# DeltaNet cores with full 128x128 inverses, built in two steps, and memory keys and values kept in DRAM between uses

## The chip, the cores and the metric

The kernel runs on one core of a Trainium2 chip. The metric is device time in microseconds (us). The profile is one more execution of the program, taken by the hardware profiler; its lines number the file of the kernel that was profiled.

## The reference

Two layers of a decoder trunk over 256 tokens with 2048 features, all in f32. Layer 0 mixes tokens with an mLSTM, layer 1 with a gated DeltaNet; each then attends to 256 memory tokens (4 heads of 128) and runs a dense MLP of width 8192 with squared ReLU. Each of the six sub-layers is `x + RMSNorm(f(RMSNorm(x)))`. What the change touches is the DeltaNet (32 value heads, 16 key heads, dimension 128, chunks of 64 tokens) and the attention's keys and values, which are made once from `mem` and used in both layers:

```python
A = jnp.einsum('...id,...jd->...ij', kb, kc) * jnp.exp(jnp.where(strict, diff, -jnp.inf))
U = lax.linalg.triangular_solve(A, vb, left_side=True, lower=True, unit_diagonal=True)
W = lax.linalg.triangular_solve(A, kb * jnp.exp(gam)[..., None], left_side=True, lower=True, unit_diagonal=True)
...
def step(Sst, xs):
    u_, w_, qg_, kd_, aqk_, dl_ = xs
    vn = u_ - jnp.einsum('bhld,bhde->bhle', w_, Sst)
    o = jnp.einsum('bhld,bhde->bhle', qg_, Sst) + jnp.einsum('bhls,bhse->bhle', aqk_, vn)
    Sst = dl_[..., None, None] * Sst + jnp.einsum('bhld,bhle->bhde', kd_, vn)
    return Sst, o
```

With 256 tokens the kernel needs no state: each head solves one unit lower triangular system over the tokens and multiplies the solution by the lower triangle of decayed q k products.

## The kernel before

**The work as a whole.** Nearly all of it is products of a 256-token activation with weights that are streamed from DRAM. Class `Weights` loads units of 512x512 (or 2048x128, "tall") in two halves on SP's queue (L74), rounds each on ACT (`hi`, L88) and takes the rest on DVE (`lo`, L89); TensorE (PE) then runs three products per block, hi·hi, lo·hi and hi·lo. Two units are kept ahead, in two buffers each of `hi` and `lo`. `prod_tok` (L378 to L380) has tokens in the output's partitions, `prod_feat` and `prod_tall` features.

**Order.** The program is written as one sequence; a scheduler then puts the instructions of each engine in an order of their own, by its estimate of when each can run. Each engine works its list off strictly in order. `behind` adds an order without a wait.

**The DeltaNet.** Stage gd1 makes q, k and the decays, and for each group of 4 value heads (8 groups) the matrices `at`: for each head three 128x128 blocks of the key system (token half 0 with itself, half 1 with itself, half 0 to half 1) and three of the query products. They go to DRAM (`at_d`), and the 32x32 diagonal blocks of the key system to `a_d`. Stage gd2 makes v, and beside it `solve` inverts the 32x32 blocks on DVE, all at once, one block a partition (`tm`); inverses go to DRAM as `t_d`, laid out in 64x64 with a zero off-diagonal quarter, and a transposed copy of the first of each pair to `tn_d`.

Stage gd3 is where the change works. For each group `core(grp, zs, ys)` runs behind the product gz of that group (`prod_tok`, 96 matmuls of 128x512, four weight units). Partitions are the 128 tokens of a half, `c2` is the chunk of 64 in it, `tt` the half, `hh` the head in the group. A core before:

- Loads, on POOL's queue: `vt` (values; L1083), `ti` (inverses, two loads; L1087), `ab` (the `at` matrices; one buffer, L1089), `tn` (one buffer, two loads; L1096).
- `np` (L1103, 16 matmuls 64x64 with 32 columns), a scaling on DVE (L1105), `xp` (L1114, 16 matmuls 32x32), two copies on ACT (L1118): this completes each 64x64 inverse.
- Then block substitution over the four chunks: `wp` (L1145) is the 64x64 inverse times the chunk's values, copied into `vt` on ACT (L1148); `cp` is what a solved chunk takes off the next one, within a half with 64x64 matmuls (L1139), from half 0 to half 1 with 128x128 ones (L1131); `minus` (L1124) subtracts it on DVE.
- `op` (L1156, 12 matmuls of 128x128) is the output; then a norm, the gate `zs`, four transposes `otp` (L1179), and the split of the result for the product g_out.

The scheduler has put gz matmuls of the next group between the steps of a core, so that PE works while ACT and DVE evacuate.

**Keys and values of the memory.** `kmT` (L522) and `vm` (L523) are made at the start and stay in two tiles of the pool `const` until the attention of layer 1; `cross` reads them at `xs` (L751) and `xop` (L775).

Of the kernel before, what the change touches and what calls it, by code (L numbers as in the profile page):

```python
# [7 lines left out]
F32 = mybir.dt.float32  # L8
F32R = mybir.dt.float32r
AF = mybir.ActivationFunctionType  # L10
ALU = mybir.AluOpType
# [3 lines left out]
P = 128  # L15
# [95 lines left out]
def trunk(ctx: ExitStack, tc, x, mem, norm_g, mem_norm_g, w_mem_kv, w_xq, w_xo, w_up, w_down,  # L111
# [295 lines left out]
    def new_u(n=KB):  # L407
        return [acts.tile([P, 2 * T], F32R, tag=f"u{k}", name=f"u{k}") for k in range(n)]
# [438 lines left out]
    def gdn(g0, h, rms):  # L847
# [4 lines left out]
        tn_d = tc.dram_tile([P, 64, 32], F32, name="tn_d")  # L852
# [175 lines left out]
        with tc.tile_pool(name="gd2", bufs=1) as sc:  # L1028
            def solve():


                rki = sc.tile([P, 2, 1, 32], F32, name="rki")
                nc.gpsimd.dma_start(rki, rk_d.rearrange("r v (c i) -> (r v c) i", c=2))
                tm = sc.tile([P, 64, 64], F32, name="tm")
                clear = G.memset(tm, 0.0)
                G.memset(tm.rearrange("p c i -> p (c i)")[:, 0:4096:65], 1.0)
                work = g0.tile([P, 2560], F32, tag="at", name="solve_w")
                am = work[:, 0:2048].rearrange("p (s j i) -> p s j i", s=2, j=32)
                pv = work[:, 2048:].rearrange("p (s c) -> p s c", s=2)
                zero = acts.tile([P, 32, 32], F32, tag="y1", name="zero")  # L1040
# [18 lines left out]
                tn = acts.tile([P, 32, 32], F32, tag="y0", name="tn")  # L1059
                S.copy(tn, td[0].rearrange("p c i -> p i c"))  # L1060
                nc.gpsimd.dma_start(tn_d[:, 0:32, :], tn)


            solver, steps = solve(), {3: 12, 4: 8, 5: 6, 6: 6}
            next(solver)
            for c in range(2, 8):
                prod_v(c)
                n = steps.get(c, 0)
                try:
                    for i in range(n):  # L1070
                        solver.send(padded[i * 4 // n - 4])
                except StopIteration:
                    pass
                store_v(c - 1)
        gp_stack.close()

        with tc.tile_pool(name="gd3", bufs=1) as sc:
            post = Post(1, 1)

            def core(grp, zs, ys):  # L1080

                vt = sc.tile([P, 2, 512], F32, tag="vt", bufs=2, name="vt")
                nc.gpsimd.dma_start(vt, v_d[grp])  # L1083
                ti = sc.tile([P, 2, 4, 64], F32, tag="ti", bufs=2, name="ti")
                for tt in range(2):
                    base = (tt * GV_H + grp * 4) * 2
                    nc.gpsimd.dma_start(ti[:, tt], t_d[base : base + 8].rearrange("(g c) j i -> (c j) g i", c=2))  # L1087
                ab = g0.tile([P, 6, 4, P], F32, tag="at", name="ab")
                nc.gpsimd.dma_start(ab, at_d[grp])  # L1089
                aa, aq = ab[:, 0:3], ab[:, 3:6]  # L1090
                w = vt

                tn = sc.tile([P, 2, 4, 32], F32, tag="tn", name="tn")
                for tt in range(2):
                    base = (tt * GV_H + grp * 4) * 2
                    nc.gpsimd.dma_start(tn[:, tt], tn_d[base : base + 8].rearrange("(g c) i j -> (c i) g j", c=2))  # L1096
                np_ = psum("np")
                for tt in range(2):
                    for c2 in range(2):
                        r_ = slice(c2 * 64, c2 * 64 + 64)  # L1100
                        for hh in range(4):
                            c = (tt * 4 + hh) * 32
                            PE.matmul(np_[r_, c : c + 32], aa[r_, tt, hh, r_], tn[r_, tt, hh, :],  # L1103
                                      start=(tt == 0 and hh == 0), stop=(tt == 1 and hh == 3), skip_group_check=True)
                V.tensor_tensor(tn.rearrange("p t (k v) i -> p t k (v i)", k=2),  # L1105
                                np_[:, 0:T].rearrange("p (t k i) -> p t k i", t=2, k=2),
                                nrk[:, :, grp * 2 : grp * 2 + 2].unsqueeze(3).to_broadcast([P, 2, 2, 64]), ALU.mult)
                xp = psum("xp")
                for tt in range(2):
                    for c2 in range(2):  # L1110
                        r1, r2 = slice(c2 * 64, c2 * 64 + 32), slice(c2 * 64 + 32, c2 * 64 + 64)
                        for hh in range(4):
                            c = (tt * 4 + hh) * 32
                            PE.matmul(xp[r1, c : c + 32], tn[r2, tt, hh, :], ti[r2, tt, hh, 32:64],  # L1114
                                      start=(tt == 0 and hh == 0), stop=(tt == 1 and hh == 3), skip_group_check=True)
                for c2 in range(2):
                    r1 = slice(c2 * 64, c2 * 64 + 32)
                    S.copy(ti[r1, :, :, 32:64], xp[r1, 0:T].rearrange("p (t h i) -> p t h i", t=2, h=4))  # L1118

                def minus(r_, tt, cp):  # L1120
                    for kh in range(2):
                        s_ = slice(kh * T, kh * T + T)
                        hk = grp * 2 + kh
                        V.scalar_tensor_tensor(vt[r_, tt, s_], cp[r_, s_], nrk[r_, tt, hk : hk + 1], vt[r_, tt, s_],  # L1124
                                               ALU.mult, ALU.add)

                for tt in range(2):
                    if tt == 1:
                        cp = psum("cp")
                        for hh in range(4):  # L1130
                            PE.matmul(cp[:, hh * P : (hh + 1) * P], aa[:, 2, hh, :], w[:, 0, hh * P : (hh + 1) * P],  # L1131
                                      start=(hh == 0), stop=(hh == 3), skip_group_check=True)
                        minus(slice(0, P), 1, cp)
                    for c2 in range(2):
                        r_ = slice(c2 * 64, c2 * 64 + 64)
                        if c2 == 1:
                            cp = psum("cp")
                            for hh in range(4):
                                PE.matmul(cp[64:128, hh * P : (hh + 1) * P], aa[0:64, tt, hh, 64:128],  # L1139
                                          w[0:64, tt, hh * P : (hh + 1) * P], start=(hh == 0), stop=(hh == 3),  # L1140
                                          skip_group_check=True)
                            minus(r_, tt, cp)
                        wp = psum("wp")
                        for hh in range(4):
                            PE.matmul(wp[r_, hh * P : (hh + 1) * P], ti[r_, tt, hh, :],  # L1145
                                      vt[r_, tt, hh * P : (hh + 1) * P], start=(hh == 0), stop=(hh == 3),
                                      skip_group_check=True)
                        S.copy(w[r_, tt, :], wp[r_])  # L1148

                ops = []  # L1150
                ss = sc.tile([P, 2, 4], F32, tag="ss", bufs=2, name="ss")
# [86 lines left out]
```

## Time and profile before

| | us |
|---|---|
| median of 3 runs | 2954.86 |
| lowest and highest run | 2952.91, 2958.61 |
| the profiled execution | 2962.7 |
| its span | 2960.6 |
| PE busy in it | 2911.2 (98%) |
| DVE busy | 1746.1 (59%) |
| ACT busy | 1443.7 (49%) |

The page lists busy time by engine (PEld is PE's loading of the stationary operand), the chain of work that ended last, groups of instructions by line, and DMA issues. In a line of the chain or the timeline the first number is the start in us from the beginning of the span, the second the length; `<-` names what was waited for. A busy PE isn't PE at its peak.

### The profile page before, as it was taken

Reading aid. Unit: us, or ns where it says so; the run is one execution under the profiler, and the core shown is the slowest. Engines: PE = TensorE matmul, PEld = TensorE weight load, DVE = VectorE, ACT = ScalarE, POOL = GpSimd, SP = SyncE. Lnnn points to the kernel's source line nnn. Section 1 sums busy time; section 2 is a strip of 40 time slices with the busy share of each in tenths; the row PEclk is TensorE's granted clock in tenths of the full one; section 3 lists DMA queues with packets and bytes.
Section 4 is the critical chain, followed back from the end, with each engine's and each line's share of the span. In section 5 each row is a group of like instructions: output and inputs, shape, how many; then the busy total and the mean of one; then the engine's idle time right before and its main releaser. Section 6 shows DMA issues by size and latency. Waiting matters only on the chain.

```text
span 2960.6 us, 42191 instructions
## 1 busy us (share of the span) xinstructions
PE 2911.2 (98%) x16595; PEld 2504.0 (85%) x16595; DVE 1746.1 (59%) x2544; ACT 1443.7 (49%) x2213; POOL 137.1 (5%) x256
## 2 busy tenths in 40 slices
PE   8999999999999999999999999999999999999998
PEld 7888888988888888898889977877888888888887
DVE  5555657654645555677778844444567546455565
ACT  6444546544434444566664544444456444344343
POOL 0000000000000000013321011000000000000000
PEclk9999999999999999999999999999999999999999
DMA  7545565556655556556778755655445565555565
GB/s 232 178 157 158 192 199 167 168 186 194 189 189 187 193 186 196 180 150 167 204 204 226 240 200 182 212 182 172 162 149 185 186 197 185 191 191 189 188 190 170
DMA packets 373960, 553.15 MB, mean 187 GB/s; under 512 B 22769, under 2 KB 155378, under 8 KB 371458
## 3 DMA queue, kind: packets, MB, share of 16 engines
q1 hardware_dynamic: 363456, 507.12, 55.1%
q0 software_dynamic: 8736, 42.02, 4.1%
q8 instruction: 130, 2.13, 0.3%
q10 hardware_dynamic: 1570, 1.33, 0.1%
q14 instruction: 68, 0.56, 0.1%
HBM read 527.29 MB, written 23.10 MB: 186 GB/s over the span
## 4 chain that ended last, share of the span: by engine, by line
PE 92%; DMA 3%; DVE 3%; ACT 1%; issue 1%; DVEq 0%; ACTq 0%; SPq 0%
PE up L314 15%; PE up L315 8%; PE down L378 8%; PE down L380 8%; PE down L379 8%; DMA raw<-in_gdn_w_in 2%; PE gz L378 2%; PE gz L380 2%; PE gz L379 2%; PE g_out L378 2%; PE g_out L380 2%; PE g_out L379 2%; PE o L314 2%; PE gv L335 2%; PE gv L333 2%; PE gv L334 2%
## 5 line engine op out<-in xcount | busy, mean ns | idle before, releaser
L89 DVE TENSOR_TENSOR lo<-raw,hi 128x1024 fp32r<-128x1024 f32 x938 | 1121.4, 1224 | 901.3 <-ACT hi L88 900.4
L88 ACT CAST hi<-raw 128x1024 fp32r<-128x1024 f32 x938 | 947.6, 1046 | 972.2 <-PE down L380 310.8
L314 PE MATMUL up<-h,hi 128*128 128x512 f32 x1920 | 678.7, 399 | 0.0
L315 PE MATMUL up<-h,lo 128*128 128x256 f32 x1920 | 539.2, 281 | 0.0
L314 PEld LDWEIGHTS up<-h,hi 128*128 128x128 f32 x1920 | 360.8, 188 | 89.8
L379 PE MATMUL down<-lo,u 128*128 128x512 f32 x1024 | 398.4, 389 | 0.0
L378 PE MATMUL down<-hi,u 128*128 128x512 f32 x1024 | 398.4, 389 | 0.0
L380 PE MATMUL down<-hi,u 128*128 128x512 f32 x1024 | 398.3, 389 | 0.0
L315 PEld LDWEIGHTS up<-h,lo 128*128 128x128 f32 x1920 | 362.7, 189 | 0.2
L380 PEld LDWEIGHTS down<-hi,u 128*128 128x128 f32 x1024 | 192.2, 188 | 40.0
L378 PEld LDWEIGHTS down<-hi,u 128*128 128x128 f32 x1024 | 192.2, 188 | 40.0
L379 PEld LDWEIGHTS down<-lo,u 128*128 128x128 f32 x1024 | 192.2, 188 | 39.6
L333 PE MATMUL gv<-h,hi 128*128 128x256 f32 x512 | 148.6, 290 | 1.7 <-ACT hi L88 1.7
L335 PE MATMUL gv<-h,lo 128*128 128x256 f32 x512 | 147.9, 289 | 0.8 <-DVE lo L89 0.8
L334 PE MATMUL gv<-h,hi 128*128 128x256 f32 x512 | 147.6, 288 | 0.0
L378 PE MATMUL gz<-hi,h 128*128 128x512 f32 x256 | 103.7, 405 | 0.0
L380 PE MATMUL gz<-hi,h 128*128 128x512 f32 x256 | 103.0, 402 | 0.0
L333 PEld LDWEIGHTS gv<-h,hi 128*128 128x128 f32 x512 | 100.7, 197 | 2.7 <-ACT hi L88 2.3
L379 PE MATMUL gz<-lo,h 128*128 128x512 f32 x256 | 102.5, 400 | 0.0
L335 PEld LDWEIGHTS gv<-h,lo 128*128 128x128 f32 x512 | 100.6, 197 | 1.5 <-DVE lo L89 1.5
L334 PEld LDWEIGHTS gv<-h,hi 128*128 128x128 f32 x512 | 100.8, 197 | 0.3 <-issue 0.2
L378 PE MATMUL g_out<-hi,u 128*128 128x512 f32 x256 | 100.9, 394 | 0.0
(412 smaller groups left out, 4728.4 us busy)
## 6 DMA issues: line engine op xcount, KB each, us to landing
raw<-in_w_up SPq DMA_DIRECT2D x256, 512.0 KB, 3.9
raw<-in_w_down SPq DMA_DIRECT2D x256, 512.0 KB, 4.2
raw<-in_gdn_w_in SPq DMA_DIRECT2D x192, 512.0 KB, 4.9
raw<-in_mlstm_w_in SPq DMA_DIRECT2D x96, 512.0 KB, 4.0
raw<-in_gdn_w_out SPq DMA_DIRECT2D x64, 512.0 KB, 4.2
raw<-in_mlstm_w_out SPq DMA_DIRECT2D x32, 512.0 KB, 4.4
at_d<-at POOLq DMA_DIRECT2D x8, 1536.0 KB, 7.6
ab<-at_d POOLq DMA_DIRECT2D x8, 1536.0 KB, 8.6
```

What stands on the lines that cost most here:

```text
L88: a = nc.scalar.copy(h_, raw[:, :, :n])
L89: return a, nc.vector.tensor_tensor(l_, raw[:, :, :n], h_, ALU.subtract)
L314: PE.matmul(a[:fw], wh, srcs[kk][:, :], start=(kk == 0), stop=False, skip_group_check=True)
L315: PE.matmul(a[:fw, T:], wl, srcs[kk][:, 0:T], start=False, stop=(kk == nk - 1), skip_group_check=True)
L333: PE.matmul(a[:, 0:T], hi[k], srcs[k][:, 0:T], start=(k == 0), stop=False)
L334: PE.matmul(a[:, 0:T], hi[k], srcs[k][:, T:], start=False, stop=False)
L335: m = PE.matmul(a[:, 0:T], lo[k], srcs[k][:, 0:T], start=False, stop=(k == nk - 1))
L378: PE.matmul(accs[t], sh, hi[j], start=(kk == 0), stop=False)
L379: PE.matmul(accs[t], sh, lo[j], start=False, stop=False)
L380: PE.matmul(accs[t], sl, hi[j], start=False, stop=(kk == nk - 1))
```

## The change

Instead of substituting over four chunks, each core completes the inverse of a whole half (128 tokens) and applies it once. The quarter step fills the 32x32 off-diagonal block of each 64x64 inverse (np, xp, now with 32x32 matmuls, and for the first chunk also its transposed form), the half step the 64x64 off-diagonal block of the 128x128 inverse (np, xp, 64 columns, eight matmuls each). wp is then one block of four 128x128 matmuls for each half, and only the cp from half 0 to half 1 is left. The full inverses lie in two tiles `tf` that are kept for the stage, with the lower left blocks cleared once; `tn` gets two buffers and four loads, `tf` four loads.

To make room, `kmT` and `vm` are stored to DRAM after they are made and their pool is closed; `cross` loads them into tiles of its own. The rest of the diff:

```diff
-    kmT = const.tile([P, XA_H, T], F32, name="kmT")
-    vm = const.tile([P, 2, 512], F32, name="vm")
+    km_d = tc.dram_tile([P, XA_H * T], F32, name="km_d")
+    vm_d = tc.dram_tile([P, 2 * 512], F32, name="vm_d")
+    kv_stack = ExitStack()
+    kv = kv_stack.enter_context(tc.tile_pool(name="kv", bufs=1))
+    kmT = kv.tile([P, XA_H, T], F32, name="kmT")
+    vm = kv.tile([P, 2, 512], F32, name="vm")
...
+    nc.gpsimd.dma_start(km_d, kmT.rearrange("p h m -> p (h m)"))
+    nc.gpsimd.dma_start(vm_d, vm.rearrange("p m d -> p (m d)"))
+    kv_stack.close()
...
     def cross(sc, l, h, rms):
...
+        kmT = sc.tile([P, XA_H, T], F32, bufs=1, name="kmT")
+        nc.gpsimd.dma_start(kmT.rearrange("p h m -> p (h m)"), km_d)
+        vm = sc.tile([P, 2, 512], F32, bufs=1, name="vm")
+        nc.gpsimd.dma_start(vm.rearrange("p m d -> p (m d)"), vm_d)
...
-                nc.gpsimd.dma_start(tn_d[:, 32:, :], zero)
+                nc.gpsimd.dma_start(tn_d[:, 0:32, 32:], zero)
+                nc.gpsimd.dma_start(tn_d[:, 32:, 0:32], zero)
...
-                S.copy(tn, td[0].rearrange("p c i -> p i c"))
-                nc.gpsimd.dma_start(tn_d[:, 0:32, :], tn)
+                for i in range(2):
+                    S.copy(tn[i], td[i].rearrange("p c i -> p i c"))
+                    r_ = slice(i * 32, i * 32 + 32)
+                    nc.gpsimd.dma_start(tn_d[:, r_, r_], tn[i])
...
+            tfs = [sc.tile([P, 2, 4, P], F32, name=f"tf{i}") for i in range(2)]
+            for tf in tfs:
+                G.memset(tf[64:, :, :, 0:64], 0.0)
...
+                        nc.gpsimd.dma_start(tf[r_, tt, :, r_],
+                                            t_d[base : base + 8].rearrange("(g c) j i -> c j g i", c=2)[c2])
...
-                            PE.matmul(np_[r_, c : c + 32], aa[r_, tt, hh, r_], tn[r_, tt, hh, :],
+                            PE.matmul(np_[q2[c2], c : c + 32], aa[q1[c2], tt, hh, q2[c2]], tn[q1[c2], tt, hh, 0:32],
...
+                        for c2 in range(2):
+                            t2 = tf[q2[c2], tt, hh, q2[c2]]
+                            PE.matmul(xp[q1[c2], c : c + 32], na_[q2[c2], c : c + 32], t2, **at_end)
+                        PE.matmul(xp[q2[0], c : c + 32], tf[q2[0], tt, hh, q2[0]], na_[q2[0], c : c + 32], **at_end)
+                x4 = lambda r_: xp[r_, 0:T].rearrange("p (t h i) -> p t h i", t=2, h=4)
+                V.tensor_copy(tn[q2[0], :, :, 0:32], x4(q2[0]))
                 for c2 in range(2):
+                    S.copy(tf[q1[c2], :, :, q2[c2]], x4(q1[c2]))
+                np_ = psum("np")
+                xp = psum("xp")
+                for tt in range(2):
+                    for hh in range(4):
+                        c = (tt * 4 + hh) * 64
+                        PE.matmul(np_[half[1], c : c + 64], aa[half[0], tt, hh, half[1]], tn[half[0], tt, hh, :],
+                                  start=(tt == 0 and hh == 0), stop=(tt == 1 and hh == 3), skip_group_check=True)
+                na_ = tmp.tile([P, 512], F32, tag="pair", bufs=3, name="na")
+                V.tensor_tensor(na_[half[1]].rearrange("p (t k i) -> p t k i", t=2, k=2),
+                                np_[half[1]].rearrange("p (t k i) -> p t k i", t=2, k=2),
+                                nrk[half[1], :, grp * 2 : grp * 2 + 2].unsqueeze(3).to_broadcast([64, 2, 2, P]), ALU.mult)
...
+                        PE.matmul(xp[half[0], c : c + 64], na_[half[1], c : c + 64], tf[half[1], tt, hh, half[1]],
+                                  start=(tt == 0 and hh == 0), stop=(tt == 1 and hh == 3), skip_group_check=True)
+                S.copy(tf[half[0], :, :, half[1]], xp[half[0]].rearrange("p (t h i) -> p t h i", t=2, h=4))
...
-                    for c2 in range(2):
-                        r_ = slice(c2 * 64, c2 * 64 + 64)
-                        if c2 == 1:
-                            cp = psum("cp")
...
-                                PE.matmul(cp[64:128, hh * P : (hh + 1) * P], aa[0:64, tt, hh, 64:128],
...
-                            PE.matmul(wp[r_, hh * P : (hh + 1) * P], ti[r_, tt, hh, :],
-                                      vt[r_, tt, hh * P : (hh + 1) * P], start=(hh == 0), stop=(hh == 3),
-                                      skip_group_check=True)
-                        S.copy(w[r_, tt, :], wp[r_])
+                    wp = psum("wp")
+                    for hh in range(4):
+                        PE.matmul(wp[:, hh * P : (hh + 1) * P], tf[:, tt, hh, :], vt[:, tt, hh * P : (hh + 1) * P],
+                                  start=(hh == 0), stop=(hh == 3), skip_group_check=True)
+                    S.copy(w[:, tt, :], wp)
```

The order of the instructions outside the cores is the same on PE, and nearly so on the other engines. Three places differ in a way that matters. The first is PE in the second core, from the cp between the halves to op. Before (the numbers tell buffers apart; hi and lo with one number are one weight unit):

```order
L1131 MATMUL cp<-vt,ab 128x128 x4
L380 MATMUL gz_1_16329<-hi_16148,h_10277 128x512
L378 MATMUL gz_1_16329<-hi_16148,h_10278 128x512
L379 MATMUL gz_1_16329<-lo_16149,h_10278 128x512
L1145 MATMUL wp<-vt,ti 64x128 x4
```

And in the change:

```order
L378 MATMUL gz_0_16366<-hi_16368,h_10293 128x512
L1170 MATMUL cp<-vt,ab 128x128 x4
L379 MATMUL gz_0_16366<-lo_16369,h_10293 128x512
L380 MATMUL gz_0_16366<-hi_16368,h_10293 128x512
L378 MATMUL gz_0_16366<-hi_16368,h_10294 128x512
L379 MATMUL gz_0_16366<-lo_16369,h_10294 128x512
L380 MATMUL gz_0_16366<-hi_16368,h_10294 128x512
L378 MATMUL gz_0_16366<-hi_16368,h_10295 128x512
L379 MATMUL gz_0_16366<-lo_16369,h_10295 128x512
L380 MATMUL gz_0_16366<-hi_16368,h_10295 128x512
L1179 MATMUL wp<-vt,tf_15744 128x128 x4
L1189 MATMUL op<-vt,ab 128x128 x12
```

Three gz matmuls lay between cp and the next wp; now eight do, the first of a new weight unit lies before cp, and op follows the second wp in one piece.

The second is DVE in the same core, from the scaling of np (lo is a weight split). Before:

```order
L1105 TENSOR_TENSOR tn<-np,nrk 128x256
L89 TENSOR_TENSOR lo_16331<-raw_0_16332,hi_16330 128x1024
L89 TENSOR_TENSOR lo_16331<-raw_2_16334,hi_16330 128x1024
L1124 SCALAR_TENSOR_TENSOR vt<-cp,nrk,vt 64x256 x2
L1124 SCALAR_TENSOR_TENSOR vt<-cp,nrk,vt 128x256 x2
L1124 SCALAR_TENSOR_TENSOR vt<-cp,nrk,vt 64x256 x2
```

And in the change:

```order
L1131 TENSOR_TENSOR na<-np,nrk 32x256 x2
L89 TENSOR_TENSOR lo_16369<-raw_0_16370,hi_16368 128x1024
L1145 COPY tn<-xp 32x8x32
L89 TENSOR_TENSOR lo_16369<-raw_2_16372,hi_16368 128x1024
L1156 TENSOR_TENSOR na<-np,nrk 64x512
L89 TENSOR_TENSOR lo_16403<-raw_0_16404,hi_16402 128x1024
L1175 SCALAR_TENSOR_TENSOR vt<-cp,nrk,vt 128x256 x2
L89 TENSOR_TENSOR lo_16403<-raw_2_16406,hi_16402 128x1024
```

Both splits of a unit stood together before the first subtraction; now one stands ahead of each of three steps of the core, the last of them (unit 16403) ahead of the subtraction between the halves.

The third is ACT at the end of layer 0's attention, where the norm's statistics of xo are taken (junk is the square's unused result, rpost the norm's factor). Before:

```order
L228 ACTIVATE junk,sspost<-xo_1_4430 128x512
L88 CAST hi_4493<-raw_0_4495 128x1024
L228 ACTIVATE junk,sspost<-xo_0_4491 128x512
L481 ACTIVATE rpost<-rpost,eps_t 128x1
L228 ACTIVATE junk,sspost<-xo_1_4492 128x512
```

And in the change:

```order
L911 ACT_TABLE_LOAD
L911 ACTIVATE na<-na 128x32
...
L88 CAST hi_4507<-raw_0_4509 128x1024
L228 ACTIVATE junk,sspost<-xo_0_4505 128x512
L481 ACT_TABLE_LOAD
L481 ACTIVATE rpost<-rpost,eps_t 128x1
```

The exponential of gdn_a_log (na), which stood in the mLSTM before, has moved into this place; a table load stands ahead of it and another one right ahead of rpost.

More of the change, by code (lines that the diff above doesn't have):

```diff
@@ L851, in gdn @@
         a_d = tc.dram_tile([P, 2, 32, 32], F32, name="a_d")
-        tn_d = tc.dram_tile([P, 64, 32], F32, name="tn_d")
+        tn_d = tc.dram_tile([P, 64, 64], F32, name="tn_d")
         t_d = tc.dram_tile([P, 64, 64], F32, name="t_d")
@@ L1083, in core @@
                 nc.gpsimd.dma_start(vt, v_d[grp])
-                ti = sc.tile([P, 2, 4, 64], F32, tag="ti", bufs=2, name="ti")
+                tf = tfs[grp % 2]
+                tn = sc.tile([P, 2, 4, 64], F32, tag="tn", bufs=2, name="tn")
+                half = [slice(c2 * 64, c2 * 64 + 64) for c2 in range(2)]
                 for tt in range(2):
                     base = (tt * GV_H + grp * 4) * 2
-                    nc.gpsimd.dma_start(ti[:, tt], t_d[base : base + 8].rearrange("(g c) j i -> (c j) g i", c=2))
+                    for c2 in range(2):
+                        r_ = half[c2]
+                        nc.gpsimd.dma_start(tf[r_, tt, :, r_],
+                                            t_d[base : base + 8].rearrange("(g c) j i -> c j g i", c=2)[c2])
+                        n_ = slice(c2 * 64, c2 * 64 + (32 if c2 else 64))
+                        nc.gpsimd.dma_start(tn[n_, tt, :, 0 : n_.stop - n_.start], tn_d[base : base + 8].rearrange(
+                            "(g c) i j -> c i g j", c=2)[c2][0 : n_.stop - n_.start, :, 0 : n_.stop - n_.start])
                 ab = g0.tile([P, 6, 4, P], F32, tag="at", name="ab")
@@ L1091, in core @@
                 w = vt
[L1093 to L1096, printed above, removed]
+                q1 = [slice(c2 * 64, c2 * 64 + 32) for c2 in range(2)]
+                q2 = [slice(c2 * 64 + 32, c2 * 64 + 64) for c2 in range(2)]
                 np_ = psum("np")
                 for tt in range(2):
-                    for c2 in range(2):
-                        r_ = slice(c2 * 64, c2 * 64 + 64)
-                        for hh in range(4):
+                    for hh in range(4):
+                        for c2 in range(2):
@@ L1108, in core @@
+                for c2 in range(2):
+                    V.tensor_tensor(na_[q2[c2]].rearrange("p (t k i) -> p t k i", t=2, k=2),
+                                    np_[q2[c2], 0:T].rearrange("p (t k i) -> p t k i", t=2, k=2),
+                                    nrk[q2[c2], :, grp * 2 : grp * 2 + 2].unsqueeze(3).to_broadcast([32, 2, 2, 64]),
+                                    ALU.mult)
                 xp = psum("xp")
                 for tt in range(2):
[L1110 to L1115, printed above, removed]
@@ L1116, in core @@
-                for c2 in range(2):
[L1117 to L1125, printed above, removed]
+                    for hh in range(4):
+                        c = (tt * 4 + hh) * 32
+                        at_end = dict(start=(tt == 0 and hh == 0), stop=(tt == 1 and hh == 3), skip_group_check=True)
+                        for c2 in range(2):
+                            t2 = tf[q2[c2], tt, hh, q2[c2]]
+                            PE.matmul(xp[q1[c2], c : c + 32], na_[q2[c2], c : c + 32], t2, **at_end)
+                        PE.matmul(xp[q2[0], c : c + 32], tf[q2[0], tt, hh, q2[0]], na_[q2[0], c : c + 32], **at_end)
```

27 lines of the change are left out of this document (13 added, 14 removed).

## The prediction

> **What bounds the kernel now.** First the page's head.
>
> ```profile
> span 2960.6 us, 42191 instructions
> PE 2911.2 (98%) x16595; PEld 2504.0 (85%) x16595; DVE 1746.1 (59%) x2544; ACT 1443.7 (49%) x2213; POOL 137.1 (5%) x256
> ```
>
> Then the windows view for the stretch in which the edited code runs (its columns: length, then for PE, PEld, DVE, ACT and POOL the busy time with its count, then granted clock, DMA share and GB/s).
>
> ```profile
> 1720.00:2130.00 410.00, 410.00 (x2491) 324.85 (x2490) 199.46 (x306) 190.45 (x259) 27.65 (x41) 1.00 0.53 178
> ```
>
> From 1720 to 2130 us PE never rests, its clock is whole, DVE and ACT are busy for less than half of the time and the DMA engines for 53%. So in this stretch time is what PE is given to do, in its order. What a core gives it stands in the chain of waits (start, length, what); here the longest pieces around the second core.
>
> ```profile
> 1758.27 1.36 PE np L1103 x32
> 1760.53 0.82 PE xp L1114 x32
> 1762.47 1.01 PE wp L1145 x8
> 1764.62 1.01 PE cp L1139 x8
> 1769.47 0.89 PE cp L1131 x8
> 1771.05 1.01 PE wp L1145 x8
> 1773.21 1.01 PE cp L1139 x8
> 1776.91 0.86 PE op L1156 x6
> 1778.01 1.56 PE op L1156 x14
> 1795.31 1.36 PE np L1103 x32
> ```
>
> Core follows core every 1795.31 - 1758.27 = 37.04 us, and between the blocks lie matmuls of the next gz product. The trace counts two records for each matmul of the program (np: 16 in the order, x32 here); I count records. The same chain asked for this stretch alone has the shorter pieces.
>
> ```profile
> 1759.63 0.43 PE gz L378
> ...
> 1770.36 0.23 PE gz L380
> ...
> 1775.69 0.64 PE op L1156 x4
> 1776.33 0.58 PE wp L1145 x4
> ```
>
> The first gz matmul behind a block on a part of the array costs 0.43 us (behind np, at 1759.63); behind the full 128x128 block it is 0.23 (1770.36), as between gz matmuls. So a change back from a small shape costs 0.20 us. Neither this view nor the waits list has PE waiting for DVE or ACT at a core: the gz matmuls between the blocks cover those round trips. Only weight loads stand for a moment:
>
> ```profile
> PEld wp L1145 <- DVE vt L1124: 8.7, 24, 0.4
> ```
>
> 24 stops of 0.36 us each, and 0.20 of that is the shape change.
>
> **The change part by part.** *Removed from PE in each core.* np 1.36; xp 0.82; wp in two blocks of 1.01 and four of 0.58 (in the order: 4, 2, 2, 4, 2, 2 matmuls), 4.34; the diagonal cp (L1139) 2 x 1.01 = 2.02; eight changes back from a small shape (behind np, xp, four blocks of wp and two of cp, where gz follows) 8 x 0.20 = 1.60; op in three pieces 0.64 + 0.86 + 1.56 = 3.06, since two blocks of wp stand inside it. Sum 13.20 us.
>
> *Added.* Quarter step, 16 matmuls np and 24 xp, all 32x32 with 32 columns: 80 records. The row of the same shape is xp: 0.82 / 32 = 25.6 ns a record. There the two halves of the array change every four matmuls; the new order changes at nearly each, so more may run side by side. Ends: 12.8 ns (two always together), 1.02 us; 42.5 ns (np: 1.36 / 32), 3.40 us. I take 22 ns, near the row of the same shape: 1.76 us. Half step, 8 np and 8 xp of 64x64 with 64 columns: 32 records. Ends: np's 42.5 ns (64x64, 32 columns), 1.36 us, and wp's 1.01 / 8 = 126 ns (64x64, 128 columns), 4.03 us; 64 columns lie a third of the way, 70 ns: 2.24 us. The two full wp blocks are the shape of the cp at 1769.47: 2 x 0.89 = 1.78. op stands in one block of 24 records at 1.56 / 14 = 111 ns: 2.67. Five changes back (np, xp's first matmul, the rest of xp, the half np and xp): 1.00. Sum 9.45 us. The 128x128 cp and the transposes stay.
>
> So 3.75 us less in each of eight cores: 30.0 us. With both ends low it would be 13.20 - 7.83 = 5.37 (43.0 us in all), with both high 13.20 - 12.88 = 0.32 (2.6 us).
>
> On the quarter step the Trainium skill speaks with two voices. "TensorE: Matmul & The Clock Gate", in "Wait — 56ns, not 53.3ns?", says that start to start never drops below about 25 ns; by that the 80 records cost 2.0 us, and the change brings 28 us. The same page in "Part 3: Packing small matmuls — row/col tiling" says that matmuls on different row groups start about 4 ns apart and run together; by that they cost near 1.0 us and the change brings 36. The 25.6 ns of xp stand at the first rule, but its blocks alternate too seldom to refute the second.
>
> *Does the cover hold?* The chain inside a core changes: np, xp, np, xp, wp, cp, wp, op, each waiting for DVE or ACT in between, against np, xp and seven turns of wp and cp before op. It is shorter, but on DVE a split of weights (lo) now stands ahead of three of its steps. The durations:
>
> ```profile
> 1759.67 0.42 DVE L1105 TENSOR_TENSOR tn<-np,nrk 128x256 f32<-128x256 f32 x1 [3.31 <-PE np L1103]
> 1760.01 2.35 DVE L89 TENSOR_TENSOR lo<-raw,hi 128x1024 fp32r<-128x1024 f32 x2
> ...
> 1770.40 0.88 DVE L1124 SCALAR_TENSOR_TENSOR vt<-cp,nrk,vt 128x256 f32<-128x256 f32 x2 [3.83 <-PE cp L1131]
> ```
>
> ```profile
> 1763.52 0.58 ACT L1148 COPY vt<-wp 64x512 f32<-64x512 f32 x1 [1.39 <-PE wp L1145]
> ...
> 1772.58 1.99 ACT L88 CAST hi<-raw 128x1024 fp32r<-128x1024 f32 x2
> ```
>
> The tightest place is behind the full cp. The last gz matmul of a weight unit stands right before cp and frees the hi buffer; then ACT casts (1.99 / 2 = 1.00), DVE splits (2.35 / 2 = 1.18), and only then half of vt can run (0.44): 2.62 us. PE has cp and eight gz matmuls to fill that, 0.89 + 8 x 0.23 = 2.73. Handing over isn't in the 2.62, so I take 0.1 us a core for a short stop, 0.8 us in all; if the cover is gone, the full price is a rival below. At the other steps the cover is wider: np to xp has three gz matmuls as before, with the same 0.42 of DVE for the first half of np; xp to np five, np to xp seven, xp to wp and wp to cp four, as wp to cp had. The two small copies on ACT of xp's quarters become three copies, off PE, on an engine busy 190 of 410 us.
>
> *POOL's queue and the loads.* A core's loads grow from six to ten (tf four, tn four).
>
> ```profile
> 1740.41 1.48 POOL L1087 DMA_DIRECT2D ti<-t_d  x2 [14.29 <-PE wp L1145]
> 1742.83 0.55 POOL L1089 DMA_DIRECT2D ab<-at_d  x1 [0.94 <-PE op L1156]
> ```
>
> ```profile
> ab<-at_d POOLq DMA_DIRECT2D x8, 1536.0 KB, 8.6
> ```
>
> ab has one buffer, is issued behind the last use by op and lands 8.6 us later, at 1751.4; the core that reads it starts at 1758.27, 6.9 us later. Now four loads of tf wait ahead of it for the last wp: 2 x 0.74 = 1.5 us more of POOL, and the next core comes 3.75 earlier. 1.6 us are left even if op comes no earlier, so I cost it at nothing; without that cover the gain of a core would go where the ab load ends. The four loads of tn go ahead of tf and need only the half np.
>
> *Outside the cores.* Keys and values: two stores and two loads of 512 KB in each layer's attention, on POOL, before first use.
>
> ```profile
> 271.53 0.86 PE np L689 x4
> 476.48 1.73 PE xs L751 x8
> ...
> 2087.29 1.56 PE op L1156 x14
> 2184.72 0.84 ACT hi L88
> 2195.12 1.73 PE xs L751 x8
> ```
>
> The memory comes free behind the last head (271.53) or core (2087.29), the first reader is xs at 476.48 or 2195.12: over 100 us of cover each, cost nothing. The solver's transposing copy on ACT becomes two, and its stores to tn_d four instead of two, on POOL.
>
> ```profile
> 1669.17 2.01 ACT L1060 COPY tn<-tm 128x1024 f32<-128x1024 f32 x1
> ```
>
> A weight cast queued behind it comes 2.01 us later; PE takes its weights two units ahead there, so I cost it at nothing, and at most 2.0 us once if that lead is spent. The same room for keys and values moves the exponential of gdn_a_log, with a table load ahead of it, into the tail of the first attention, so that the square root of rpost has to load its table again:
>
> ```profile
> 499.60 1.28 ACT L463 ACT_TABLE_LOAD   x1
> ...
> 515.08 0.30 ACT L481 ACTIVATE rpost<-rpost,eps_t 128x1 f32<-128x1 f32 x1 [0.78 <-DVE rpost L479]
> ```
>
> ACT idles 0.78 us there, the load takes 1.28: 0.5 us on a path on which PE stands until the residual. Sum: 30.0 - 0.8 - 0.5 = 28.7 us less. The profiled run took 2962.7 us (its span and 2.1 around it), 7.8 above the median of the runs, 2954.86; I take the 28.7 off the median: 2926.2.
>
> **The rivals.** *The small shapes are dearer than their rows* (a change of place at each 32x32 matmul costs something, 64 columns cost near what 128 do). For it: no row has that alternation. Both high ends give 2.6 us less; half-way between that and my sum, 16 us, 2939. *They run fully side by side*: both low ends, 43.0 - 1.3 = 42 us, 2913. For it: xp's 25.6 ns is already below np's 42.5. *The splits on DVE hold PE* (slower): lo stands ahead of COPY tn, of the half na and of vt; where a core's hi cast comes late by itself, each of the three can hold PE for a cast and a split, 1.00 + 1.18 = 2.18, 6.5 us a core, 52 in all; less the 28.7, 2978. It decides from 3.6 us of stops in each core on. Against it: hi and lo find their data (DMA 53% here), DVE idles 3.31 and 3.83 us before its core steps. *Another resource sets the pace, so that the change doesn't do what it says*: ab's load or the weight stream keeps the 37.04 us period, or PE's stops give back nearly all: 2955. Against it: the 6.9 us of ab and the DMA share.
>
> **How the numbers follow.** Forecast 0.77 (2919 to 2934 by itself), small shapes dearer 0.08, side by side 0.08, splits hold PE 0.03, another pace 0.04. A measurement of this kernel tells about 0.2% (6 us) from no change. Faster: 0.77 + 0.08 + 0.08 = 0.93; same 0.04; slower 0.03. The range takes in the side-by-side case whole at 2913 and the dearer one to 2940; what is beyond on either side is under 2 in 10.
>
> **What would show it.** Right: core to core 33.3 us in the chain; full wp at 0.89 a block or joined with op; the half np and xp near 1.1 us each; no wait of PE for DVE at wp; ab landing before the next np. Wrong: a period over 35 us; PE waiting at wp for vt, or at np for ab; a shape change behind wp; a wait for kmT at xs.

## The result, and the profile after

The changed kernel takes 2936.78 us (median of 4 runs, 2932.73 to 2937.61), the kernel before on the same chip 2954.66 (4 runs, 2952.91 to 2958.61): a ratio of 0.9941, 95% interval 0.9929 to 0.9953. That is 17.4 us less by the ratio (0.0059 x 2954.66), 17.9 by the medians, where 28.7 were forecast. The profiled execution took 2937.6 us, span 2935.6.

The page's head of the changed kernel:

```profile
span 2935.6 us, 42499 instructions
PE 2879.0 (98%) x16723; PEld 2487.2 (85%) x16723; DVE 1744.7 (59%) x2536; ACT 1445.0 (49%) x2207; POOL 161.2 (5%) x298
```

PE's busy time fell by 2911.2 - 2879.0 = 32.2 us, the span by 25.0. This span can't be set against the first profile of before as it stands: before's profiled execution was 7.8 us over its median, and a second profile of it, e0 below, has a span of 2953.3. The stretch of the cores, in the windows view:

```profile
1720.00:2130.00 410.00, 410.00 (x2760) 335.75 (x2759) 214.60 (x313) 202.97 (x268) 40.55 (x69) 1.00 0.61 200
```

PE is still never idle there and its clock is whole. The chain of waits around the second core, after:

```profile
1760.49 0.62 PE np L1127 x32
1762.01 0.17 PE xp L1142 x2
1762.84 0.14 PE xp L1142
...
1763.46 0.01 PE xp L1143
1764.83 1.07 PE np L1153 x16
1767.72 1.07 PE xp L1162 x16
1769.91 0.89 PE wp L1179 x8
1771.72 0.91 PE cp L1170 x8
1774.48 1.12 PE wp L1179 x8
1775.60 2.68 PE op L1189 x24
...
1797.87 1.07 PE np L1153 x16
```

From half np to half np it is 1797.87 - 1764.83 = 33.04 us, where it was 37.04: 4.0 us less a core. The second wp is 0.23 longer than the first, and one row of the weight loads' waits says why; beside it the loads of ab and of tf:

```profile
PEld wp L1179 <- DVE vt L1175: 3.1, 8, 0.4
```

```profile
ab<-at_d POOLq DMA_DIRECT2D x8, 1536.0 KB, 8.1
tf<-t_d POOLq DMA_DIRECT2D x32, 64.0 KB, 4.2
```

Eight stops for vt, one in each core, and no wait of PE for ab in any. So the cores did what was said of them, and more. The difference to the forecast lies at the end of the triangular solver, where `gv`, the in-projection's product for v, is computed. POOL and ACT there, after (start, length, what, and in brackets the idle time ahead and what ended it):

```profile
1670.61 0.54 POOL L1071 DMA_DIRECT2D t_d<-tm  x1 [0.41 <-DVE pad L876]
1672.63 1.71 POOL L1075 DMA_DIRECT2D tn_d<-tn  x1 [1.48 <-ACT tn L1073]
1674.59 1.70 POOL L1075 DMA_DIRECT2D tn_d<-tn  x1 [0.25 <-ACT tn L1073]
...
1677.41 0.54 POOL L1116 DMA_DIRECT2D ab<-at_d  x1
```

```profile
1670.31 3.98 ACT L1073 COPY tn<-tm 128x1024 f32<-128x1024 f32 x2
...
1693.19 1.04 ACT L88 CAST hi<-raw 128x1024 fp32r<-128x1024 f32 x1 [9.64 <-DMA raw<-in_gdn_w_in]
```

ACT makes its copies (3.98 us, before 2.01), and after two copies of v and four casts it stands 9.64 us for a weight of the in-projection. The chain of waits has that transfer with what stood ahead of it, the waits list has what PE lost, and the windows have the clock (its column is the third from the right):

```profile
1672.23 2.05 ACT tn L1073
...
1675.64 0.96 ACT hi L88
1676.63 1.24 DVE lo L89
1677.88 15.21 DMA raw<-in_gdn_w_in
```

```profile
PE gv L333 <- ACT hi L88: 5.4, 2, 4.9
```

```profile
1690.00:1700.00 10.00, 5.07 (x23) 4.77 (x24) 4.57 (x7) 4.39 (x7) 0.00 (x0) 0.73 0.90 307
1700.00:1710.00 10.00, 10.00 (x59) 9.06 (x59) 7.28 (x11) 5.01 (x8) 3.40 (x7) 0.93 0.72 212
```

A weight that lands in 4.9 us by the median over the whole kernel took 15.21; PE waited 4.9 us for its cast; and behind the wait the granted clock is 0.73. A slice of 10 us in which gv runs at the whole clock has 86 matmul records, 0.116 us each; the 23 records in 5.07 us cost 2.4 us more than that, and the next slice, at 0.93, holds some more. That the clock falls behind such a wait is what the Trainium skill says ("TensorE: Matmul & The Clock Gate", Part 1: half rate after an idle window of about 3.4 us); this trace agrees, with 4.9.

The 15.21 us are not the loss by themselves, since this weight was slow before too. The second profile of the kernel before, e0, has it in its chain with 13.80 us; ahead of it the store of the inverses to `t_d`, from POOL's timeline:

```profile
1663.05 0.54 POOL L1058 DMA_DIRECT2D t_d<-tm  x1 [0.41 <-DVE tm L1056]
```

```profile
1664.66 1.06 ACT hi L88
1665.74 0.43 DVE lo L89
1666.88 0.11 DVE cv L870
1666.99 13.80 DMA raw<-in_gdn_w_in
```

Counted from the start of that store, the weight is asked for at 3.94 us in e0 and at 7.27 in the change (1677.88 - 1670.61), and it lands at 17.7 and 22.5. Of the 4.7 us between the two, 3.3 come from the later request, which waits for the cast and the split that free its buffer, both behind ACT's copies, and 1.4 from the longer transfer. PE's stop here isn't new either. The waits list of before has it (in all, times, longest; 0.5 is the longest in e0):

```profile
PE gv L333 <- ACT hi L88: 1.7, 2, 1.2
```

What the stages gained and lost, from the starts of the first matmul of three stages in the traces: the last `gq` in layer 1, the first `gz`, and the cross attention's `xq` behind the cores.

| profiled run | gq to gz, us | gz to xq, us | xq to the end, us |
|---|---|---|---|
| before, first profile | 278.2 | 475.6 | 786.7 |
| before again (e0) | 273.3 | 475.6 | 788.0 |
| after | 284.5 | 443.8 | 787.3 |

The cores gained 31.8 us. The stretch with the solver's end lost 6.3 against one profile of before and 11.2 against the other. The rest of the difference to e0 lies ahead of these stages: that `gq` starts at 1416.3 us in e0, but at 1420.1 in the first profile of before and 1420.0 in the changed kernel.

### The profile page after: what moved, and what is told of

Its sections match the earlier page's. It is cut to its first block, busy times and chain, and to the rows that moved or that the text cites. A ratio compares the mean times of both kernels' runs of the same rounds, so it can differ in the third digit from the quotient of the medians.

```text
span 2935.6 us, 42499 instructions
## 1 busy us (share of the span) xinstructions
PE 2879.0 (98%) x16723; PEld 2487.2 (85%) x16723; DVE 1744.7 (59%) x2536; ACT 1445.0 (49%) x2207; POOL 161.2 (5%) x298
## 4 chain that ended last, share of the span: by engine, by line
PE 87%; DVE 5%; DMA 4%; ACT 2%; issue 2%; DVEq 0%; ACTq 0%; SPq 0%
PE up L314 15%; PE up L315 8%; PE down L379 8%; PE down L378 8%; PE down L380 8%; DMA raw<-in_gdn_w_in 3%; PE gz L378 2%; PE gz L380 2%; PE gz L379 2%; PE g_out L380 2%; PE g_out L378 2%; PE g_out L379 2%; PE o L314 2%; DVE lo L89 2%; ACT hi L88 1%
## 5 line engine op out<-in xcount | busy, mean ns | idle before, releaser
L333 PEld LDWEIGHTS gv<-h,hi 128*128 128x128 f32 x512 | 100.1, 195 | 6.6 <-ACT hi L88 6.3
L378 PE MATMUL g_out<-hi,u 128*128 128x512 f32 x256 | 100.7, 393 | 0.0
L380 PE MATMUL g_out<-hi,u 128*128 128x512 f32 x256 | 100.4, 392 | 0.0
```

What stands on the lines that cost most here:

```text
L333: PE.matmul(a[:, 0:T], hi[k], srcs[k][:, 0:T], start=(k == 0), stop=False)
L378: PE.matmul(accs[t], sh, hi[j], start=(kk == 0), stop=False)
L380: PE.matmul(accs[t], sl, hi[j], start=False, stop=(kk == nk - 1))
```

## The experiments

Each run stands against the kernel before on the same chip, with ratio and 95% interval; "us" behind a ratio is the ratio's distance from 1 times 2954.66. **My theory**: the new stores to `tn_d` (runs of 128 bytes, from two blocks instead of one) fill the DMA engines at the moment at which `gv` needs its next weight, so ACT's cast is late and PE waits and then runs at the lower clock. **Rivals**: the second copy on ACT alone delays the casts; or the loss is elsewhere (the trips of keys and values, the table load), or it is chance between executions.

**e0, before again.** No edit.

> The kernel before once more, for a second profile of it. The first profiled execution took 2962.7 us, 8 above the median of its runs, and that of the change 2937.6, 1 above. If the 8 us were chance of that execution, this one is near 2955, and its stages show where the 8 us lay; if the profiler adds them to this kernel, it is near 2962 again. The timed rounds are the same as before, ratio 1.000.

2954.92 us, ratio 1.0005 (0.9996 to 1.0014), span of the profiled execution 2953.3. So the 7.8 us of the first profile were chance of that execution. Its granted clock was 0.83 between 1690 and 1700 us, just where the change does its damage, which is why a comparison with that profile alone hides nearly half of the loss.

**e2, before with the change's solver end alone.** Two copies, two stores of `tn` and two of `zero` into a 64x64 layout; the cores as before.

```diff
-        tn_d = tc.dram_tile([P, 64, 32], F32, name="tn_d")
+        tn_d = tc.dram_tile([P, 64, 64], F32, name="tn_d")
...
-                S.copy(tn, td[0].rearrange("p c i -> p i c"))
-                nc.gpsimd.dma_start(tn_d[:, 0:32, :], tn)
+                for i in range(2):
+                    S.copy(tn[i], td[i].rearrange("p c i -> p i c"))
+                    r_ = slice(i * 32, i * 32 + 32)
+                    nc.gpsimd.dma_start(tn_d[:, r_, r_], tn[i])
```

> The kernel before with only the change's solver end (second copy on ACT, stores of quarters and of zeros in 128-byte runs); the cores are as before. Theory DMA: 5 to 6 us slower than before, 2960, all of it between the end of the solver and the first gz, with PE waiting for a cast. Theory noise: the 6 us between the two profiles are one execution's chance, and this is at 2955 as before. By theory ACT it is slower too, by 2 us at most.

2963.46 us, ratio 1.0036 (1.0023 to 1.0048): 10.6 us slower (6.8 to 14.2), more than expected. Its waits list and its chain have the same rows as those of the changed kernel:

```profile
PE gv L333 <- ACT hi L88: 5.4, 3, 4.7
```

```profile
1669.46 15.04 DMA raw<-in_gdn_w_in
```

So this part alone brings the wait, without anything of the cores.

**e3, before with the trips of keys and values alone.**

```diff
+    nc.gpsimd.dma_start(km_d, kmT.rearrange("p h m -> p (h m)"))
+    nc.gpsimd.dma_start(vm_d, vm.rearrange("p m d -> p (m d)"))
+    kv_stack.close()
...
+        kmT = sc.tile([P, XA_H, T], F32, bufs=1, name="kmT")
+        nc.gpsimd.dma_start(kmT.rearrange("p h m -> p (h m)"), km_d)
```

> The kernel before with one part of the change alone: the memory keys and values go to DRAM after the key work and come back ahead of the cross attention; cores and solver as before. My theory (these trips are hidden, and the load of ACT's exp table that moves ahead of rpost is at most 0.5 us): 2954 to 2956 us, ratio 0.9995 to 1.0005, and no wait for kmT or vm at xs. Rival (the two loads or the table load hold a chain that the profile of after does not name): 2 us or more over before, ratio 1.0007 or more.

2954.97 us, ratio 1.0006 (0.9997 to 1.0014): 1.8 us slower, between 0.9 less and 4.1 more. The two expectations met at this size, and the run doesn't decide between them. Its trace has no wait for kmT or vm at xs. The table load stands in ACT's timeline of the changed kernel where it was expected:

```profile
514.11 1.28 ACT L481 ACT_TABLE_LOAD   x1
515.41 0.29 ACT L481 ACTIVATE rpost<-rpost,eps_t 128x1 f32<-128x1 f32 x1
```

**e4, after without the turns.** The quarter step's matmuls in the order of their place in the array, so that the place changes less often; the same matmuls.

```diff
-                    for hh in range(4):
-                        for c2 in range(2):
+                    for c2 in range(2):
+                        for hh in range(4):
```

The xp loop is turned in the same way.

> The change with the quarter step's matmuls ordered by place (all of one place, then the next) instead of changing place at each matmul; the same matmuls, only their order on PE differs. If matmuls on different places run side by side, np's 32 records go from 0.62 us back to about 0.82 and xp's 48 from about 0.9 to 1.25, 0.5 us a core, 4 us in all: 2941. If the turns don't matter, the same 2937; if each turn cost something, less than 2937.

2942.30 us, ratio 0.9965 (0.9953 to 0.9977), 7.1 us over the changed kernel by the ratios, 5.5 by the medians. Its chain at the second core:

```profile
1760.00 0.82 PE np L1127 x32
1761.72 0.36 PE xp L1143 x8
...
1765.08 1.07 PE np L1155 x16
...
1793.81 0.82 PE np L1127 x32
```

np takes 0.82 instead of 0.62 us and the period is 33.81 (from np to np) instead of 33.04, so the turns are worth 0.77 us a core, 6 in all (0.5 a core was expected).

**e1, after with plain stores.** `tn_d` holds the two 32x32 blocks apart, each stored contiguously; no zeros are stored, since the tiles that take the loads are zeroed once. The two copies on ACT stay. There are three loads of tn for each half instead of two.

```diff
-        tn_d = tc.dram_tile([P, 64, 64], F32, name="tn_d")
+        tn_d = tc.dram_tile([2, P, 32, 32], F32, name="tn_d")
...
-                    nc.gpsimd.dma_start(tn_d[:, r_, r_], tn[i])
+                    nc.gpsimd.dma_start(tn_d[i], tn[i])
```

> The change with its transposed inverses stored as two arrays of whole 32x32 blocks (4 KB runs) instead of quarters of a 64x64 array (128-byte runs), without the stores of zeros; ACT's second copy stays. Theory DMA: the short runs keep the DMA engines about 6 us longer at the end of the solver (packets of tn_d near 450 ns instead of 180), the weights of gv land late, and PE loses that once; so here PE's wait for a cast in gv falls from 4.9 us to about 1, gz starts 4 to 6 us earlier, and the time is 2931 to 2933. Theory ACT: the loss is the second copy of 2.0 us ahead of the casts; then gz starts as late as in the change and the time stays at 2937.

2928.99 us, ratio 0.9918 (0.9905 to 0.9932): 7.8 us under the changed kernel by the medians, 6.8 by the ratios. The transfer of the two stores, first after, then e1 (issue to landing, median):

```profile
tn_d<-tn POOLq DMA_DIRECT2D x2, 512.0 KB, 15.4
```

```profile
tn_d<-tn POOLq DMA_DIRECT2D x2, 512.0 KB, 7.8
```

and e1's wait and clock:

```profile
PE gv L333 <- ACT hi L88: 2.4, 2, 1.8
```

```profile
1680.00:1690.00 10.00, 7.68 (x43) 7.19 (x43) 4.51 (x7) 4.34 (x7) 0.00 (x0) 0.72 0.90 263
```

So the stores carry most of the loss. The weight is asked for as late as in the changed kernel (7.26 us behind the start of t_d's store), but takes 12.21 us instead of 15.21. A part of the gain may come from the zeros, which e1 doesn't store: behind them PE stops for lo in gv of the changed kernel, 0.76 us at 1570.5 and 0.41 at 1586.4, and at neither place in e0 or e1. A wait of 1.8 us and a drop of the clock are left.

**e7, after with the two copies on POOL**, the stores unchanged, and **e8, e1 with the two copies on POOL**. The edit is one line in both:

```diff
-                    S.copy(tn[i], td[i].rearrange("p c i -> p i c"))
+                    G.tensor_copy(tn[i], td[i].rearrange("p c i -> p i c"))
```

> The kernel after with one edit: the two copies of the solver's diagonal blocks are made on POOL instead of ACT (4 us there by the profile of e6_late_ab_pool_copy); the stores of 128-byte runs stay. Theory (the stores hold the weight back, ACT waits for the weight 9.6 us with its copies long made): no more than 2 us under 2936.8, and gv still waits 3 us or more for hi at the solver's end. Rival (the two ACT copies put the casts of the weight back by 4 us, the buffers of raw come free that much later, and that is the loss): 5 us or more under 2936.8, and the wait of gv is 2 us or less.

2931.72 us, ratio 0.9931 (0.9919 to 0.9944), 5.1 us under the changed kernel by the medians and 3.0 by the ratios, between the two expectations; the wait of 3.5 us is the first one's. ACT and the waits list of e7:

```profile
1694.99 1.04 ACT L88 CAST hi<-raw 128x1024 fp32r<-128x1024 f32 x1 [7.58 <-DMA raw<-in_gdn_w_in]
```

```profile
PE gv L333 <- ACT hi L88: 4.1, 2, 3.5
```

Without a copy on ACT, ACT still stands 7.58 us for the weight and PE 3.5. The copies are a part of the loss, by these values the smaller one, though the intervals of e1 and e7 overlap. The edit also moves the stores, since POOL makes the copies ahead of them: the first store to tn_d starts 4.5 us behind t_d's (1676.78 - 1672.26) instead of 2.0, so the run isn't one of the copies alone.

> The kernel of e1_block_stores (plain stores, ab issued early) with the two copies on POOL. Together with e1 (2929.0), e5 (2926.8: ab late) and e6 (2922.0: ab late, copies on POOL) it says whose the 4.8 us between e5 and e6 are. If the copies on ACT cost by themselves: about 2924, with gv's wait for hi at the solver's end under 1 us. If they cost only together with the late ab, whose weight for gz was then missed: 2928 to 2929, and gv's wait of 2 us or so stays.

2927.67 us, ratio 0.9911 (0.9896 to 0.9926), 2.1 us under e1 by the ratios, which the intervals don't tell apart; PE's longest wait for hi at gv is 1.3 us instead of 1.8. That is the second of the two expectations, nearly: the copies alone bring little here.

**e5, e1 with ab issued later.** The first core's load of ab (1.5 MB), which POOL issues right behind the solver's stores, is put behind the stores of v at position 6.

```diff
-                nc.gpsimd.dma_start(ab, at_d[grp])
+                d_ = nc.gpsimd.dma_start(ab, at_d[grp])
+                if grp == 0:
+                    behind(d_, vdma[13])
```

> The kernel of e1_block_stores with one order changed: the first core's ab load, 1.5 MB, is issued behind the stores of v at position 6 instead of together with the solver's last stores, so that the in-projection's weight for gv comes in with less beside it. Theory (the weight comes late because everything that is issued at the solver's end shares 16 engines): gv's first matmul waits 1 us or less for hi instead of 2.4, the granted clock does not drop at 1680 to 1700, and the time is 2 to 4 us under e1's 2929.0, that is 2925 to 2927. Rival (the solver's own 2 MB of t_d and tn_d alone hold the weight back, and ab comes behind the weight in any case): no change, 2928 to 2930.

2926.82 us, ratio 0.9907 (0.9893 to 0.9921), 3.2 us under e1 by the ratios, within the expected 2 to 4, though the intervals overlap. gv's longest wait is 0.5 us and the clock stays whole from 1680 to 1700: as the theory has it. But a new wait stands behind the late ab, at gz; the waits list and the chain of e5:

```profile
PE gz L378 <- ACT hi L88: 0.9, 1, 0.9
PE gz L379 <- DVE lo L89: 0.8, 1, 0.8
```

```profile
1691.53 10.78 DMA raw<-in_gdn_w_in
1702.33 1.05 ACT hi L88
1703.41 1.24 DVE lo L89
1704.69 0.69 PE gz L379
1705.38 0.43 PE gz L380
...
1708.37 0.23 PE gz L378
```

The chain also shows what the clock does to a matmul: gz costs 0.43 instead of 0.23 us from 1705.38 to 1708.37, seven matmuls, 1.4 us more, behind a wait of 0.9 and 0.8.

**e6, e5 with the two copies on POOL** (the edit of e7 and e8).

> The kernel of e5_late_ab with the two copies of the solver's diagonal blocks (2.0 us each on ACT) on POOL instead. Theory (the copies matter only where hi, on ACT, has its weight already and stands behind them): 1 us or less from e5's time, either way. Rival (the second ACT copy is what delays hi and so PE, the 2.0 us at most that the prediction allowed): 2 us under e5's time.

2921.99 us, ratio 0.9892 (0.9879 to 0.9905), 4.8 us under e5 by the medians, 4.4 by the ratios; I had expected 1 at most. Neither wait is left; the waits list has nothing of gz, and of gv:

```profile
PE gv L333 <- ACT hi L88: 0.5, 1, 0.5
```

So the theory fell in one point: copies and transfers don't add up one by one. I read it so that the 4 us of copies on ACT put its casts behind, and with them the time at which a buffer of raw comes free and the next weight is asked for, so that this weight falls into the next burst of transfers. The traces bear out the first half: behind the start of t_d's store the late weight is asked for at 7.26 us in e1 and e5, at 5.71 in e8 and e6, and at 3.94 in e0. The second half, the burst that it then meets, no run shows by itself. With either half of that taken away (e5, e8) a wait stayed at one of two places; with both gone none did. The stretches of all these traces, as in the table above:

| profiled run | gq to gz, us | gz to xq, us | ratio |
|---|---|---|---|
| e0 before again | 273.3 | 475.6 | 1.0005 |
| e2 before + solver end | 282.1 | 475.6 | 1.0036 |
| e3 before + keys and values | 274.5 | 475.6 | 1.0006 |
| after | 284.5 | 443.8 | 0.9941 |
| e4 no turns | 284.9 | 449.9 | 0.9965 |
| e7 copies on POOL | 283.2 | 443.9 | 0.9931 |
| e1 plain stores | 278.2 | 443.8 | 0.9918 |
| e8 plain stores, copies on POOL | 278.1 | 444.1 | 0.9911 |
| e5 plain stores, late ab | 272.8 | 448.0 | 0.9907 |
| e6 all three | 271.6 | 444.3 | 0.9892 |

e6 is the fastest version: 31.9 us under the kernel before by its ratio (28.1 to 35.8), about what the cores give by themselves (31.8).

## Why the prediction was right in direction and 11 us short

The direction, and the reason for it, were right: PE sets the time in the stretch of the cores, and what a core gives PE less to do comes off the time.

- **The cores: 29.2 us forecast (30.0 less 0.8 of stops), 31.8 measured** (gz to xq, with the stops). By term, forecast and measured for a core: the quarter step 1.76 and 1.42 us (np 0.62, xp 0.17 + 0.63 for the many short pieces from 1762.84 to 1763.47), since it ran at 18 ns a record and not 22; the half step 2.24 and 2.14 (1.07 twice, 67 ns a record for 70); wp 1.78 and the same without its stop; op 2.67 and 2.68. The interpolation from neighbouring shapes held within 5% at the half step.
- **The stop for vt: 0.1 us a core forecast, 0.23 measured** (1.12 against 0.89), 1 us more in all. The place was right, the size low by half.
- **The two voices of the Trainium skill on the quarter step** ("TensorE: Matmul & The Clock Gate"): a mean over records decides nothing between them, since it mixes two steps. In the changed kernel's trace np's records start in pairs, 6 to 7 ns apart on two different places of the array, and 25 ns pass to the next pair: 0.62 / 32 = 19 ns is the mean. In order of place (e4) the records of one place start 31 to 32 ns apart; where two places overlap, their records are 5 to 6 ns apart, and the mean is 0.82 / 32 = 26. The section "Wait — 56ns, not 53.3ns?" gives 25 ns as the least from start to start; the steps between two places lie far under that. "Part 3: Packing small matmuls — row/col tiling" gives 4 ns between row groups; the 5 to 7 here are near it. The 25.6 ns of xp before, which the prediction put at the first rule, are such a mean too (steps of 31 to 32, 5 to 6 and 25 to 27 ns): that they met the rule was luck.
- **ab's load and the trips of keys and values: nothing forecast.** ab landed ahead of its reader in each core. For the trips, e3 leaves 1.8 us with an interval that holds zero.
- **The table load: 0.5 us forecast.** It is there, 1.28 us on ACT, but no run measured its price apart; e3's 1.8 holds it.
- **The step that failed: "A weight cast queued behind it comes 2.01 us later; PE takes its weights two units ahead there, so I cost it at nothing, and at most 2.0 us once if that lead is spent."** It priced only the copy on ACT, and its upper end was no bound. Measured, the solver's end costs 10.6 us (e2, 6.8 to 14.2). The late weight was asked for 3.3 us later than in e0, not 2.0, and landed 4.7 later. The stores were only counted ("four instead of two"), not priced: the tile's rows had become 32 of 64 columns, so each store fell into runs of 128 bytes, took 1.7 us to issue instead of 0.54 and 15.4 us to land instead of 8.3, in front of the weight. Plain stores give back 6.8 us by the ratios (e1). The copies, priced at 0 to 2.0, gave 3.0 alone (e7). And the lead was already spent: before itself waits for hi at this place, 1.2 us in its first profile and 0.5 in e0, and the first of these rows was there to read. And the longer wait brought a slower clock behind it, 2.4 us in one slice, that no term allowed for.

The account closes within its errors: 31.8 less in the cores, 10.6 more at the solver's end, 1.8 more with the trips gives 19.4 less, where 17.4 were measured with an interval of 13.9 to 21.0. Within the solver's end the shares of stores, copies, ab and clock are not settled: each pair of runs differs by little more than its intervals, and e5, e6 and e8 show that they don't simply add.

## What to carry to other kernels

A store or load that changes its layout changes its price, even at the same size: count its contiguous runs, and look at which weight or operand is in flight beside it. Where a list of waits already shows a short wait of the bounding engine at a place, its lead there is spent: what is put ahead of that wait makes it longer (4.7 us here made it 4.4 longer than in e0), and it costs more than itself where the clock falls behind it. Set a slow transfer beside the same one in the run before, not beside a median over the kernel: 15.21 us stood against 13.80 here, and the later request was the larger part. Look for the loss outside the edited stage before doubting the gain inside it, and take a second profile of the kernel before, since one execution can be off by 7.8 us where the effect is 17.4.

## What the runs showed of the hardware

- A store of 512 KB in runs of 128 bytes held POOL for 1.7 us instead of 0.54. In the trace of the changed kernel the 384 DMA packets of 4096 bytes that moved on POOL's queue between 1677 and 1693 us took 337 ns on average, in e0 the 256 between 1670 and 1675 took 174. What the store did to the weight's queue is less plain: the weight's first packet moved 4.3 us after it was asked for (1677.88 to 1682.14), but 4.0 in e0 (1666.99 to 1671.03) and 4.1 in e1 as well, so the short runs didn't make that standstill.
- The granted clock fell behind waits shorter than 3.4 us, though not behind each. It was 0.72 in the slice of e1's waits (1.8 us for hi, 0.5 for lo), 0.83 with e8's (1.3 and 0.8) and behind those in the first profile of before (1.2 and 0.8), but 1.00 in e3 with the same 1.2 and 0.8, and in e0 with 0.5 and 0.8. The rule of the Trainium skill ("TensorE: Matmul & The Clock Gate", Part 1) has half rate after an idle window of about 3.4 us. Here the measurement goes further than the rule; what decides whether a short wait is enough, no run shows.
- 32x32 matmuls with 32 columns whose places change at each matmul took 19 ns a record, in order of place 26. Records on one place started 31 to 32 ns apart, records on two different places 5 to 7.
